# Grouping the distance-bias blocks of a two-layer hybrid block on TensorE: 12 groups instead of 32 single blocks, and 86 work tiles in SBUF

## Chip, cores and metric

The kernel runs on one core of one Trainium2 chip. The metric is the device time of one execution in microseconds, the median of three runs.

## What is computed

Two layers (`DEPTH = 2`) over one sequence of 512 tokens with model width 1024. Each layer makes a projection of the normed input, three branches (latent attention "mla", a chunked state-space branch "ssd", and a top-k attention "dsa"), gates and merges them, and adds a gated per-layer embedding. The change touches only the bias of the top-k attention, which depends on nothing but `positions` and the table `rel_bias`:

```python
def t5_bucket(rel):
    n = jnp.maximum(rel, 0)
    exact = REL_BUCKETS // 2
    log_ratio = jnp.log(jnp.maximum(n, exact).astype(jnp.float32) / exact) / math.log(REL_MAX_DIST / exact)
    large = jnp.minimum(exact + (log_ratio * (REL_BUCKETS - exact)).astype(jnp.int32), REL_BUCKETS - 1)
    return jnp.where(n < exact, n, large)

def dsa_branch(q_c, k_c, v_c, q_idx, k_idx, w_idx, positions, rel_bias):
    ...
    for blk in range(s // Q_BLOCK):                     # 4 query tiles of 128
        ...
        rel = jax.nn.relu(jnp.einsum('bqhd,bkd->bqhk', q_idx[:, qs:qe], k_idx))
        index_score = jnp.einsum('bqh,bqhk->bqk', w_idx[:, qs:qe], rel)
        index_score = jnp.where(key_ids <= q_ids, index_score, -jnp.inf)
        _, sel = lax.top_k(index_score, n_sel)          # n_sel = 128
        ...
        logits = jnp.einsum('bqhd,bqkd->bhqk', q_c[:, qs:qe], k_sel) * scale
        bucket = t5_bucket(positions[:, qs:qe, None] - pos_sel)
        logits = logits + jnp.moveaxis(rel_bias[bucket], -1, 1)
        probs = jax.nn.softmax(jnp.where(valid[:, None], logits, -jnp.inf), axis=-1)
        outs.append(jnp.einsum('bhqk,bqkd->bqhd', probs, v_sel))
```

The first query tile has only 128 keys before it, so it selects all of them; the other three need the top 128 of 256, 384 and 512.

## The kernel before

**Engines and order.** Everything is written as generators in `layer`. The order of TensorE is the order in which the code is run (a manual schedule); the other engines' instructions are put in order by the framework, which sets each as early as it thinks its inputs will be there, with a priority that follows the program's order (weight loads get a priority ahead, `AHEAD`). Once set, every engine works strictly in its order, and so do the DMA issues on SP (SyncE). Working tiles of 128x512 come from a ring of `NSLOT = 80` numbered slots; PSUM has eight banks under four tags, `BANKS = dict(mm=3, lg=2, tp=2, pv=1)`.

**Weights.** A matrix is brought by a DMA on SP (L225), split into a high part by ACT (L226, `wh`) and a low part by DVE (L227, `wl`); one tile of 128x512 outputs is then 24 matmuls of 128x512: `wh` and `wl` on the high input in turn (L237, L238), then `wh` on the low input (L245).

**The bias, layer 0 only.** `rel_bias` makes the bias of all 8 heads for the causal part of the 512x512 map in 32 blocks of 16 queries, from block 31 down to 0. A block has n = 512, 384, 256 or 128 key columns, eight blocks of each. For a block there are four masks of 128 x n (row = bucket and query, 1 where the distance reaches the bucket's limit): some on ACT by Sign (L379), the others on DVE by a comparison (L381); `SIGNS = (1, 2, 4)` says how many of the four ACT makes. Twelve bf16 matmuls follow (L393): three parts of the table's steps, times four masks, each to its own 32 of the 128 partitions of one PSUM bank. ACT takes the bank out (L397, the "eviction"), SP writes it to the DRAM tensor `bias_d` (L400). The masks of the next block are made while this one is multiplied.

**Where blocks are run.** `EARLY = (2, 0, 2, 2)` blocks stand between the steps of the layer's start. `REL = (1, 3, 4, 4)` stand in the four weaves of the mla attention, `LATE = 14` in the weave that holds the top-k selection (`TOP = (3, 22)`). A weave steps its main generator n times, and after each step runs a side track as long as that track's spent cost is under its share of its total:

```python
while t[2] and t[1] < t[0] * (i + 1) / n:
    t[1] += next(t[2][0])
```

What is left of a track after the n steps is run at the end, one after another. A block tells the cost 3n/512; the weave counts 2 for each block as the total.

**The top-k stage.** `topk` runs 16 rounds on DVE over the three later query tiles (L858 finds the eight largest, L861 strikes them out), then turns each score tile into an additive mask (L865, tiles `sel`). The side work of TensorE in this weave are 24-matmul tiles (`q_c`, `gate_c`, `merge`, `br_a`).

**Its attention, `dsa`.** For each head and query tile: SP reads the bias back from `bias_d` (L876), POOL adds the mask to it (L878: the causal mask `c` for the first query tile, `sel` for the others), TensorE makes the logits (L880, L881), `softmax` runs on DVE, ACT and DVE (L549 adds bias and logits, L550 exponential on ACT, L551, L552), TensorE transposes the probabilities (L560) and multiplies them with the values (L599). These reads run ahead of their use.

Of the kernel before, what the change touches and what calls it, by code (L numbers as in the profile page):

```python
# [27 lines left out]
BF = mybir.dt.bfloat16  # L28
I32 = mybir.dt.int32
AF = mybir.ActivationFunctionType  # L30
OP = mybir.AluOpType

L, D, T = 2, 1024, 512
# [125 lines left out]
class Build:  # L159
    def __init__(self, tc, I, out, ctx, dbg=None):  # L160
# [10 lines left out]
        self.dram = pool("dram", bufs=1, space=bass.MemoryType.DRAM)  # L171
        self.free_slots = deque(range(NSLOT))
        self.todo = deque()
# [8 lines left out]
    def slot(self, dt=F32, shape=(128, 512)):  # L182
        i = self.free_slots.popleft()
        self.peak = max(self.peak, NSLOT - len(self.free_slots))
        self.n += 1
# [180 lines left out]
    def rel_bias(self):  # L366


        nc = self.nc

        def masks(blk):
            n = 128 * (blk // 8 + 1)
            k = SIGNS[(blk < 32 - sum(EARLY)) + (blk < LATE)]
            tiles = [self.slot(BF, (128, 2, 512)) for _ in range(2)]
            for i in range(4):
                g = 4 * blk + i
                m = tiles[i // 2][:, i % 2, :n]
                if i >= 4 - k:
                    nc.scalar.activation(m, self.pk[:, :n], AF.Sign, scale=-1.0, bias=self.thr[:, 1, g:g + 1])  # L379
                else:  # L380
                    nc.vector.tensor_scalar(m, self.pk[:, :n], self.thr[:, 0, g:g + 1], None, op0=OP.is_le)  # L381
            return n, k, tiles
        nxt = masks(31)
        for blk in reversed(range(32)):
            n, k, tiles = nxt
            if blk:
                nxt = masks(blk - 1)
            else:
                self.rel(self.pk)
            ps = self.ps("mm" if blk >= 32 - sum(EARLY) else "tp")  # L390
            for s in range(3):
                for i in range(4):
                    nc.tensor.matmul(ps[32 * i:32 * i + 32, :n], self.steps[s][:, int(i >= 4 - k)],  # L393
                                     tiles[i // 2][:, i % 2, :n], start=s == 0, stop=s == 2)
            self.rel(*tiles)
            e = self.slot()
            nc.scalar.activation(e[:, :n], ps[:, :n], AF.Identity, scale=8.0, bias=self.half[:, k:k + 1])  # L397
            dst = bass.AP(tensor=self.bias_d.tensor, offset=self.bias_d.offset + blk * 16 * T,
                          ap=[[T, 16], [T * T, 8], [1, n]])
            nc.sync.dma_start(dst, e[:, :n])  # L400
            self.rel(e)
            yield 3 * n / 512


    def stat_add(self, s, x, first, t=slice(0, T)):
# [728 lines left out]
    def layer(self, l, xs, s):  # L1134
# [3 lines left out]
        for _ in range(PLE0):  # L1138
            next(p, None)
        blocks(EARLY[0])  # L1140
        self.now(p)
        blocks(EARLY[1])
        p = self.ple(l, 1)
# [4 lines left out]
        for _ in range(POST[l]):  # L1148
            next(p, None)
        blocks(EARLY[2])  # L1150
        R = self.stat_rows(y)
# [9 lines left out]
        self.now(p)  # L1161
        blocks(EARLY[3])
        self.ahead = AHEAD
# [7 lines left out]
        for j in range(4):  # L1171
# [6 lines left out]
                    [(ab, 33), merge(0, 6), merge(0, 7)]][j]  # L1178
            rel = [(self.rb_block(), 2) for _ in range(REL[j])] if l == 0 else []
            self.weave(att, 16, work, rel)  # L1180
# [16 lines left out]
        work += [merge(1, m) for m in range(2)]  # L1197
        self.weave(tk, TOP[1], work, [(self.rb_block(), 2) for _ in range(LATE * (l == 0))])
        att = self.dsa(l)
# [174 lines left out]


TOP = (3, 22)
REL = (1, 3, 4, 4)
WB = (3, 3, 2)
NSLOT = 80
LAST = 3  # L1380
CHUNK = 4
FIRST = (("c_kv", 0), ("c_kv", 1), "C")
# [4 lines left out]
POST = (4, 1)  # L1387
URGENT = 300
URGENT2 = 100
EARLY = (2, 0, 2, 2)  # L1390
SIGNS = (1, 2, 4)
LATE = 14
BANKS = dict(mm=3, lg=2, tp=2, pv=1)
AHEAD = 3000

# [24 lines left out]
```

## Time and profile before

| | us |
|---|---|
| median of three runs | 1435.06 (1434.89 to 1435.16) |
| the profiled execution's own time | 1434.97 |
| span of its trace | 1433.2 |
| PE busy | 1404.6 (98%) |
| DVE busy | 1085.9 (76%) |
| ACT busy | 724.3 (51%) |
| POOL busy | 155.4 (11%) |
| mean granted TensorE clock | 0.998 |

PE is the matmul side of TensorE, DVE is VectorE, ACT is ScalarE, POOL is GpSimd, and SP issues the DMAs. All times in the trace count from the start of the span. The timeline gives an instruction's start, its duration, engine and line, what it writes and reads, the number merged into the row, and in brackets the idle time before it with what ended it. Matmuls are pipelined: a duration of 0.39 us is a latency, and what a matmul costs is the distance to the next start, 0.227 to 0.23 us at 128x512.

### The profile page before, as it was taken

Reading aid. Unit: us, or ns where it says so; the run is one execution under the profiler, and the core shown is the slowest. Engines: PE = TensorE matmul, PEld = TensorE weight load, DVE = VectorE, ACT = ScalarE, POOL = GpSimd, SP = SyncE. Lnnn points to the kernel's source line nnn. Section 1 sums busy time; section 2 is a strip of 40 time slices with the busy share of each in tenths; the row PEclk is TensorE's granted clock in tenths of the full one; section 3 lists DMA queues with packets and bytes.
Section 4 is the critical chain, followed back from the end, with each engine's and each line's share of the span. In section 5 each row is a group of like instructions: output and inputs, shape, how many; then the busy total and the mean of one; then the engine's idle time right before and its main releaser. Section 6 shows DMA issues by size and latency. Waiting matters only on the chain.

```text
span 1433.2 us, 20180 instructions
## 1 busy us (share of the span) xinstructions
PE 1404.6 (98%) x7261; PEld 1151.6 (80%) x7262; DVE 1085.9 (76%) x2227; ACT 724.3 (51%) x1384; POOL 155.4 (11%) x142
## 2 busy tenths in 40 slices
PE   6999999999999999999999999999999999999997
PEld 4878777788888788888888788888888888788886
DVE  7668886996887997654565697779988799865444
ACT  7557678525655443433345575642366554443333
POOL 1000000003120231000001000000322114110000
PEclk9999999999999999999999999999999999999999
DMA  8442322343333332543454322233333343244331
GB/s 263 145 123 82 92 84 81 117 129 113 110 114 108 114 107 82 168 142 101 132 163 129 92 72 77 93 94 92 119 108 103 116 118 118 75 130 149 118 101 61
DMA packets 67609, 162.39 MB, mean 113 GB/s; under 512 B 9237, under 2 KB 21653, under 8 KB 67509
## 3 DMA queue, kind: packets, MB, share of 16 engines
q1 hardware_dynamic: 67509, 161.11, 36.1%
q8 instruction: 57, 0.93, 0.3%
q14 instruction: 43, 0.35, 0.1%
HBM read 142.27 MB, written 13.83 MB: 109 GB/s over the span
## 4 chain that ended last, share of the span: by engine, by line
PE 89%; DVE 6%; ACT 2%; issue 1%; SPq 0%; DMA 0%; POOL 0%; DVEq 0%; ACTq 0%
PE p L245 24%; PE p L237 24%; PE p L238 24%; PE p L599 3%; PE p L560 2%; DVE wl L227 1%; PE p L1070 1%; ACT wh L226 1%; PE p L1075 1%; DVE s L253 1%; PE p L680 1%; PE p L684 1%; PE p L681 1%; PE p L393 1%; PE p L1003 1%
## 5 line engine op out<-in xcount | busy, mean ns | idle before, releaser
L237 PE MATMUL p<-s,wh 128*128 128x512 f32 (+1 forms) x1644 | 648.8, 396 | 9.1 <-ACT wh L226 7.8
L238 PE MATMUL p<-s,wl 128*128 128x512 f32 (+1 forms) x1644 | 636.6, 388 | 1.2 <-DVE wl L227 1.2
L245 PE MATMUL p<-s,wh 128*128 128x512 f32 (+1 forms) x1644 | 424.4, 390 | 0.0
L226 ACT ACTIVATE wh<-wr 128x1024 fp32r<-128x1024 f32 (+2 forms) x214 | 223.5, 1044 | 326.0 <-PE p L245 212.3
L237 PEld LDWEIGHTS p<-s,wh 128*128 128x128 f32 x1644 | 309.7, 188 | 68.9 <-ACT wh L226 7.8
L238 PEld LDWEIGHTS p<-s,wl 128*128 128x128 f32 x1644 | 309.9, 189 | 60.5 <-DVE wl L227 2.6
L245 PEld LDWEIGHTS p<-s,wh 128*128 128x128 f32 x1644 | 300.6, 188 | 60.3 <-issue 2.8
L227 DVE TENSOR_TENSOR wl<-wr,wh 128x1024 fp32r<-128x1024 f32 (+2 forms) x214 | 266.7, 1246 | 101.7 <-ACT wh L226 100.2
L550 ACT ACTIVATE s<-s,m 128x128 f32<-128x128 f32 (+3 forms) x128 | 71.5, 559 | 66.1 <-DVE m L549 65.7
L569 ACT ACTIVATE s<-p 128x256 fp32r<-128x256 f32 (+1 forms) x192 | 66.0, 344 | 60.3 <-DVE s L570 31.1
L570 DVE TENSOR_TENSOR s<-p,s 128x256 fp32r<-128x256 f32 (+1 forms) x192 | 71.8, 374 | 16.2 <-ACT s L569 14.7
L878 POOL TENSOR_TENSOR s<-s,s 128x256 f32<-128x256 f32 (+2 forms) x48 | 58.9, 1244 | 204.8 <-ACT wh L226 60.2
L1129 DVE SCALAR_TENSOR_TENSOR s<-s,p 128x512 f32<-128x512 f32 x48 | 32.6, 678 | 35.9 <-PE p L245 35.9
L560 PE MATMUL p<-c,s 128*128 128x128 f32 x320 | 56.3, 274 | 2.2 <-DVE s L552 2.2
L410 ACT ACTIVATE s<-s 128x512 f32<-128x512 f32 (+1 forms) x42 | 25.3, 609 | 65.6 <-DVE s L1096 40.9
L560 PEld LDWEIGHTS p<-c,s 128*128 128x128 f32 x320 | 40.6, 140 | 18.5 <-issue 5.6
L552 DVE TENSOR_SCALAR s<-s,m 128x128 f32<-128x128 f32 (+3 forms) x128 | 53.5, 418 | 2.5
L963 DVE SCALAR_TENSOR_TENSOR s<-p,v,s 128x511 f32<-128x511 f32 (+2 forms) x72 | 53.3, 740 | 0.0
L861 DVE MATCH_REPLACE8 s<-m,s 128x256 f32<-128x256 f32 (+2 forms) x96 | 51.6, 542 | 0.0
L858 DVE MAX8 m<-s 128x8 f32<-128x256 f32 (+2 forms) x96 | 49.2, 547 | 0.0
L252 ACT ACTIVATE s<-s 128x512 fp32r<-128x512 f32 (+1 forms) x58 | 36.3, 626 | 25.5 <-DVE s L642 10.9
L253 DVE TENSOR_TENSOR s<-s,s 128x512 fp32r<-128x512 f32 (+1 forms) x58 | 43.2, 745 | 7.1 <-ACT s L252 6.7
(199 smaller groups left out, 1634.6 us busy)
## 6 DMA issues: line engine op xcount, KB each, us to landing
wr<-in_w_dram SPq DMA_DIRECT2D x204, 512.0 KB, 3.6
s<-cum_d SPq DMA_DIRECT2D x32, 256.0 KB, 3.8
s<-in_x_dram SPq DMA_DIRECT2D x16, 256.0 KB, 4.3
ple_d<-s SPq DMA_DIRECT2D x16, 256.0 KB, 4.1
s<-bias_d SPq DMA_DIRECT2D x16, 256.0 KB, 2.7
s<-ple_d SPq DMA_DIRECT2D x13, 256.0 KB, 2.7
s<-bias_d SPq DMA_DIRECT2D x16, 192.0 KB, 2.7
s<-s SPq DMA_DIRECT2D x44, 64.0 KB, 2.0
```

The source lines that it names most:

```text
L226: nc.scalar.activation(hi[:, :n], raw[:, :n], AF.Copy)
L227: nc.vector.tensor_sub(lo[:, :n], raw[:, :n], hi[:, :n].bitcast(F32))
L237: nc.tensor.matmul(ps[:, t], hi[:, c], ah[:, t], start=k == 0, stop=False)
L238: nc.tensor.matmul(ps[:, t], lo[:, c], ah[:, t], start=False, stop=False)
L245: nc.tensor.matmul(ps[:, t], hi[:, c], al[:, t], start=False, stop=k == n - 1)
L253: self.nc.vector.tensor_sub(lo, src, hi.bitcast(F32))
L550: nc.scalar.activation(u[:, :n], u[:, :n], AF.Exp, bias=mx, scale=-1.0, accum_out=sm)
L552: nc.vector.tensor_scalar(u[:, :n], u[:, :n], rs, None, op0=OP.mult)
L560: nc.tensor.transpose(tp[:, 128 * kb:128 * kb + 128], u[:, 128 * kb:128 * kb + 128], self.ident)
L569: nc.scalar.activation(h_, src, AF.Copy)
L570: nc.vector.tensor_sub(l_, src, h_.bitcast(F32))
L878: nc.gpsimd.tensor_tensor(b[:, :n], b[:, :n], mask, OP.add)
```

## The change

`masks` and the loop work on groups of neighbouring blocks of one width instead of single blocks. `GROUPS` has eight groups of two blocks (31 to 16) and four groups of four (15 to 12, 11 to 8, 7 to 4, 3 to 0). A group's matmuls run one block after another, with as many blocks side by side in a bank as fit in 512 columns; banks are taken in turn under the tags `tp` and `mm`. A bank is taken out by one eviction whatever is in it, and written by one DMA for each block. The number of matmuls (384), masks (128) and DMAs (32) stays; the evictions go from 32 to 22. `EARLY` is one group where it was two blocks, `REL` is (1, 1, 2, 2) groups, `LATE` is 3, `EDGES` sets the widths at which ACT takes over masks (blocks 13 and 12 have now two masks on ACT instead of four), and a group tells its cost as 3n times its blocks over 512, while the weave goes on counting 2 for each. `NSLOT` is 86.

```diff
--- before.py
+++ after.py
@@ -368,38 +368,47 @@
 
         nc = self.nc
 
-        def masks(blk):
-            n = 128 * (blk // 8 + 1)
-            k = SIGNS[(blk < 32 - sum(EARLY)) + (blk < LATE)]
-            tiles = [self.slot(BF, (128, 2, 512)) for _ in range(2)]
-            for i in range(4):
-                g = 4 * blk + i
-                m = tiles[i // 2][:, i % 2, :n]
-                if i >= 4 - k:
-                    nc.scalar.activation(m, self.pk[:, :n], AF.Sign, scale=-1.0, bias=self.thr[:, 1, g:g + 1])
+        def masks(group):
+            n, k = 128 * (group[0] // 8 + 1), SIGNS[(group[0] < EDGES[0]) + (group[0] < EDGES[1])]
+            per = 1024 // n
+            tiles = [self.slot(BF, (128, 1024)) for _ in range(-(-4 * len(group) // per))]
+            at = lambda m: tiles[m // per][:, n * (m % per):n * (m % per) + n]
+            for m in range(4 * len(group)):
+                g = 4 * group[m // 4] + m % 4
+                if m % 4 >= 4 - k:
+                    nc.scalar.activation(at(m), self.pk[:, :n], AF.Sign, scale=-1.0, bias=self.thr[:, 1, g:g + 1])
                 else:
-                    nc.vector.tensor_scalar(m, self.pk[:, :n], self.thr[:, 0, g:g + 1], None, op0=OP.is_le)
-            return n, k, tiles
-        nxt = masks(31)
-        for blk in reversed(range(32)):
-            n, k, tiles = nxt
-            if blk:
-                nxt = masks(blk - 1)
+                    nc.vector.tensor_scalar(at(m), self.pk[:, :n], self.thr[:, 0, g:g + 1], None, op0=OP.is_le)
+            return n, k, tiles, at
+        nxt = masks(GROUPS[0])
+        for j, group in enumerate(GROUPS):
+            n, k, tiles, at = nxt
+            if j + 1 < len(GROUPS):
+                nxt = masks(GROUPS[j + 1])
             else:
                 self.rel(self.pk)
-            ps = self.ps("mm" if blk >= 32 - sum(EARLY) else "tp")
-            for s in range(3):
-                for i in range(4):
-                    nc.tensor.matmul(ps[32 * i:32 * i + 32, :n], self.steps[s][:, int(i >= 4 - k)],
-                                     tiles[i // 2][:, i % 2, :n], start=s == 0, stop=s == 2)
+
+            banks, side = [], 512 // n
+            for b, blk in enumerate(group):
+                if b % side == 0:
+                    banks.append(self.ps(("tp", "mm")[len(banks) % 2]))
+                ps = banks[-1][:, n * (b % side):n * (b % side) + n]
+                for s in range(3):
+                    for i in range(4):
+                        nc.tensor.matmul(ps[32 * i:32 * i + 32], self.steps[s][:, int(i >= 4 - k)], at(4 * b + i),
+                                         start=s == 0, stop=s == 2)
             self.rel(*tiles)
-            e = self.slot()
-            nc.scalar.activation(e[:, :n], ps[:, :n], AF.Identity, scale=8.0, bias=self.half[:, k:k + 1])
-            dst = bass.AP(tensor=self.bias_d.tensor, offset=self.bias_d.offset + blk * 16 * T,
-                          ap=[[T, 16], [T * T, 8], [1, n]])
-            nc.sync.dma_start(dst, e[:, :n])
-            self.rel(e)
-            yield 3 * n / 512
+            for b0 in range(0, len(group), side):
+                blks = group[b0:b0 + side]
+                e, m = self.slot(), n * len(blks)
+                nc.scalar.activation(e[:, :m], banks[b0 // side][:, :m], AF.Identity, scale=8.0,
+                                     bias=self.half[:, k:k + 1])
+                for b, blk in enumerate(blks):
+                    dst = bass.AP(tensor=self.bias_d.tensor, offset=self.bias_d.offset + blk * 16 * T,
+                                  ap=[[T, 16], [T * T, 8], [1, n]])
+                    nc.sync.dma_start(dst, e[:, n * b:n * b + n])
+                self.rel(e)
+            yield 3 * n * len(group) / 512
 
 
     def stat_add(self, s, x, first, t=slice(0, T)):
@@ -1374,9 +1383,9 @@
 
 
 TOP = (3, 22)
-REL = (1, 3, 4, 4)
+REL = (1, 1, 2, 2)
 WB = (3, 3, 2)
-NSLOT = 80
+NSLOT = 86
 LAST = 3
 CHUNK = 4
 FIRST = (("c_kv", 0), ("c_kv", 1), "C")
@@ -1387,9 +1396,13 @@
 POST = (4, 1)
 URGENT = 300
 URGENT2 = 100
-EARLY = (2, 0, 2, 2)
+
+GROUPS = [list(range(a - 1, a - 1 - k, -1)) for a, k in
+          [(32 - 2 * i, 2) for i in range(8)] + [(16, 4), (12, 4), (8, 4), (4, 4)]]
+EARLY = (1, 0, 1, 1)
 SIGNS = (1, 2, 4)
-LATE = 14
+EDGES = (26, 12)
+LATE = 3
 BANKS = dict(mm=3, lg=2, tp=2, pv=1)
 AHEAD = 3000
 
```

Lines from L411 on move by 9, so what was L878 is now L887, L876 is L885, L865 is L874, L880 is L889; the matmuls L393 are L398, the evictions L397 are L404, the writes L400 are L409.

**TensorE at the first logits of `dsa`** (`p` is PSUM, `rbp` the table's steps, `wh` and `wl` a weight's parts, `s` slots). Before:

```order
L245 MATMUL p750_3760<-s82_413,wh748_3754 128x512
L245 MATMUL p750_3760<-s85_418,wh748_3754 128x512
L245 MATMUL p750_3760<-s88_423,wh748_3754 128x512
L245 MATMUL p750_3760<-s91_428,wh748_3754 128x512
L880 MATMUL p753_3793<-s152_806,s609_2898 128x256
L881 MATMUL p753_3793<-s153_807,s609_2898 128x256
L237 MATMUL p759_3810<-s69_392,wh757_3804 128x512
L238 MATMUL p759_3810<-s69_392,wl757_3805 128x512
```

After:

```order
L398 LDWEIGHTS rbp2_119
L398 MATMUL p710_3685<-s707_3613,rbp2_119 32x128
L398 LDWEIGHTS rbp2_119
L398 MATMUL p710_3685<-s707_3613,rbp2_119 32x128
L889 MATMUL p713_3743<-s154_812,s613_3000 128x256
L890 MATMUL p713_3743<-s155_813,s613_3000 128x256
L237 MATMUL p719_3760<-s71_398,wh717_3754 128x512
L238 MATMUL p719_3760<-s71_398,wl717_3755 128x512
```

The last two groups (96 matmuls, blocks 7 to 0) now stand directly ahead of the first logits; before, 152 rows lay between the last block and the logits.

**POOL at the adds of `dsa` in layer 0** (`c_77` is the causal mask of the first query tile; the other last operands are the three top-k masks). Before:

```order
L878 TENSOR_TENSOR s752_3790<-s752_3790,c_77 128x128
L878 TENSOR_TENSOR s786_3936<-s786_3936,c_77 128x128
L878 TENSOR_TENSOR s824_4108<-s824_4108,c_77 128x128
L878 TENSOR_TENSOR s760_3823<-s760_3823,s258_1280 128x256
L878 TENSOR_TENSOR s796_3980<-s796_3980,s258_1280 128x256
L878 TENSOR_TENSOR s767_3853<-s767_3853,s259_1281 128x384
L878 TENSOR_TENSOR s778_3897<-s778_3897,s260_1282 128x512
L878 TENSOR_TENSOR s804_4021<-s804_4021,s259_1281 128x384
```

After:

```order
L887 TENSOR_TENSOR s720_3773<-s720_3773,s264_1308 128x256
L887 TENSOR_TENSOR s756_3930<-s756_3930,s264_1308 128x256
L887 TENSOR_TENSOR s727_3803<-s727_3803,s265_1309 128x384
L887 TENSOR_TENSOR s738_3847<-s738_3847,s266_1310 128x512
L887 TENSOR_TENSOR s764_3971<-s764_3971,s265_1309 128x384
L887 TENSOR_TENSOR s774_4011<-s774_4011,s266_1310 128x512
L887 TENSOR_TENSOR s793_4100<-s793_4100,s264_1308 128x256
L887 TENSOR_TENSOR s802_4145<-s802_4145,s265_1309 128x384
L887 TENSOR_TENSOR s813_4189<-s813_4189,s266_1310 128x512
L887 TENSOR_TENSOR s712_3740<-s712_3740,c_77 128x128
L887 TENSOR_TENSOR s746_3886<-s746_3886,c_77 128x128
```

The adds of the first query tile stood ahead of nine adds that read the top-k masks; now they stand behind them.

**SP at the last writes to `bias_d` and the first reads of the first query tile** (`wr` are weights; `16x8x128` is a write of one narrow block). Before:

```order
L400 DMA bias_d_146<-s693_3419 16x8x128
L400 DMA bias_d_146<-s697_3441 16x8x128
L225 DMA wr733_3662<-in_w_dram 128x1024
L400 DMA bias_d_146<-s705_3491 16x8x128
L876 DMA s752_3790<-bias_d_146 128x128
L876 DMA s786_3936<-bias_d_146 128x128
L876 DMA s824_4108<-bias_d_146 128x128
L225 DMA wr739_3705<-in_w_dram 128x1024
```

After:

```order
L225 DMA wr752_3904<-in_w_dram 128x1024
L225 DMA wr770_3989<-in_w_dram 128x1024
L885 DMA s813_4189<-bias_d_146 128x512
L225 DMA wr789_4074<-in_w_dram 128x1024
L409 DMA bias_d_146<-s709_3679 16x8x128 x4
L409 DMA bias_d_146<-s711_3734 16x8x128 x4
L885 DMA s712_3740<-bias_d_146 128x128
L885 DMA s746_3886<-bias_d_146 128x128
```

The eight narrow writes now stand together, behind weight loads that stood behind them before; the 128x128 reads stand behind all eight.

## Rows read from the trace of the kernel before

**Rows 1.** The page, busy time of each engine: us (share of the span) xinstructions.

```profile
PE 1404.6 (98%) x7261; PEld 1151.6 (80%) x7262; DVE 1085.9 (76%) x2227; ACT 724.3 (51%) x1384; POOL 155.4 (11%) x142
```

**Rows 2.** Windows: busy us of each engine, granted clock, DMA share, GB/s.

```profile
312.00:322.00 10.00, 10.00 (x46) 8.26 (x44) 10.00 (x24) 1.44 (x2) 0.34 (x1) 1.00 0.38 135
```

**Rows 3.** Timeline of PE, bias runs: the first in a weave, and the last.

```profile
106.06 0.83 PE L393 MATMUL p<-s,rbp 128*32 128x512 bf16 x12
...
292.53 0.35 PE L393 MATMUL p<-s,rbp 128*32 128x128 bf16 x12
```

**Rows 4.** Timeline of PE, a run of two narrow blocks and one of one.

```profile
276.05 0.39 PE L238 MATMUL p<-s,wl 128*128 128x512 f32 x1
276.36 0.52 PE L393 MATMUL p<-s,rbp 128*32 128x128 bf16 x24
...
277.15 0.39 PE L238 MATMUL p<-s,wl 128*128 128x512 f32 x1
...
284.65 0.39 PE L238 MATMUL p<-s,wl 128*128 128x512 f32 x1
284.96 0.35 PE L393 MATMUL p<-s,rbp 128*32 128x128 bf16 x12
...
285.59 0.40 PE L238 MATMUL p<-s,wl 128*128 128x512 f32 x1
```

**Rows 5.** Timeline of PE near the start: a wait for an eviction.

```profile
20.55 0.50 PE L237 MATMUL p<-s,wh 128*128 128x512 f32 x1 [1.08 <-ACT s L397]
```

**Rows 6.** Line L397, the evictions: count, ns min/median/max, first and last start.

```profile
L397 ACT ACTIVATE s<-p,rbh x32: 352/524/696, 17.1 to 292.9; 128x512 f32<-128x512 f32 x8, 128x384 f32<-128x384 f32 x8, 128x256 f32<-128x256 f32 x8, 128x128 f32<-128x128 f32 x8
```

**Rows 7.** Timeline of DVE: top-k's first and last instructions, then the first softmax.

```profile
252.75 0.43 DVE L858 MAX8 m<-s 128x8 f32<-128x256 f32 x1
...
321.24 0.90 DVE L865 TENSOR_SCALAR s<-s 128x256 f32<-128x256 f32 x3
...
327.98 0.29 DVE L549 CUSTOM_DVE_ANT_0 s<-p,s 128x128 f32<-128x128 f32 x1 [3.46 <-PE p L881]
...
328.73 1.23 DVE L227 TENSOR_TENSOR wl<-wr,wh 128x1024 fp32r<-128x1024 f32 x1 [0.45 <-ACT wh L226]
...
330.07 0.57 DVE L552 TENSOR_SCALAR s<-s,m 128x128 f32<-128x128 f32 x1
```

**Rows 8.** Timeline of POOL, 296 to 334 us: its bias adds.

```profile
297.95 2.28 POOL L878 TENSOR_TENSOR s<-s,c 128x128 f32<-128x128 f32 x3 [162.80 <-DMA s<-bias_d]
321.66 11.12 POOL L878 TENSOR_TENSOR s<-s,s 128x256 f32<-128x256 f32 x9 [21.43 <-issue]
```

**Rows 9.** Line L878: its first-query-tile adds, ns min/median/max.

```profile
L878 POOL TENSOR_TENSOR s<-s,c x16: 460/466/1322, 297.9 to 1101.8; 128x128 f32<-128x128 f32 x16
```

**Rows 10.** Timeline of PE: the first logits, and the first transpose of probabilities.

```profile
327.44 0.28 PE L880 MATMUL p<-s,s 128*128 128x256 f32 x1
...
332.50 0.27 PE L560 MATMUL p<-c,s 128*128 128x128 f32 x1
```

**Rows 11.** Line L400, the bias writes: ns of an issue; us from issue to landing.

```profile
L400 SPq DMA_DIRECT2D bias_d<-s x32: 517/528/790, 18.0 to 293.3; - x32
...
DMA to landing us min/median/max: 2.2/3.1/5.2
```

**Rows 12.** Line L876, the bias reads: us from issue to landing.

```profile
DMA to landing us min/median/max: 1.7/2.7/4.8
```

**Rows 13.** Timeline of PE at the start, after 7.84 us without work.

```profile
7.84 0.79 PE L237 MATMUL p<-s,wh 128*128 128x512 f32 x1 [7.84 <-ACT wh L226]
...
9.69 0.63 PE L237 MATMUL p<-s,wh 128*128 128x512 f32 x1
...
13.11 0.93 PE L245 MATMUL p<-s,wh 128*128 128x512 f32 x2
```

**Rows 14.** Timeline of PE, its last instruction.

```profile
1425.10 0.43 PE L435 MATMUL p<-c,m 128*128 128x128 f32 x2
```

**Rows 15.** Windows behind it: the column after the five engines is the granted clock.

```profile
1427.00:1427.50 0.50, 0.00 (x0) 0.00 (x0) 0.50 (x2) 0.00 (x0) 0.36 (x1) 0.50 0.00 0
```

## What the change was expected to do

> **What bounds the kernel now.** I read the page first: PE is busy for 98% of the span, DVE 76%, ACT 51%, POOL 11% [rows 1]. So a microsecond taken from TensorE's stream is worth a microsecond, unless the stream then has to wait. I then read the windows, to see whether another engine is full anywhere. In the stretch of the top-k selection DVE is busy 10.00 of 10 us [rows 2], from the first MAX8 at 252.75 to the last mask at 321.24 + 0.90 = 322.14 [rows 7], while PE is full too. That is a second chain as long as PE's: the masks come when DVE is through, however fast PE is. Last I read the timeline from the end of top-k to the first attention of `dsa`. There PE makes the first logits at 327.44 and transposes the first probabilities at 332.50 [rows 10] without idle time before it. The bias adds of the first query tile were done on POOL long before, from 297.95; the nine adds that need the masks ran from 321.66 for 11.12 us [rows 8]. So before the change the first probabilities hung on nothing late.
>
> **What is removed from PE.** In the weaves there are 23 runs of bias matmuls, the first at 106.06 and the last at 292.53 [rows 3]. The change leaves 8 there, so 15 fewer. What a run costs I read where a run of two narrow blocks and a run of one stand near each other. From the weight matmul ahead of the run to the second one behind it, two blocks take 277.15 - 276.05 = 1.10 us, one takes 285.59 - 284.65 = 0.94 [rows 4]. Without a run these two steps are 0.46, so a run of two costs 0.64, of one 0.48: each narrow block 0.16, and 0.32 for going in and out. The blocks' own time stays; 15 x 0.32 = 4.8. Runs that end at a 128-column transpose, not at a weight matmul, pay a little less on leaving, so I take 4.6, with 3.9 and 5.0 as ends. **The ten evictions less** I price at nothing: ACT is at 51% [rows 1] and its evictions run beside TensorE's weight matmuls; without that cover they would be worth 10 x 0.52 = 5.2 at the median [rows 6].
>
> **What is added: two evictions to wait for.** A group of two wide blocks fills two banks, and the next user of the second bank waits for one eviction more. Near the start PE already waits 1.08 us for an eviction [rows 5], and a 512-wide one lasts 0.67 to 0.70, the median one 0.52 [rows 6]. For the three early groups I take 0.8 together (0 to 1.4: none, or two more evictions in full). Two later groups of 384-wide blocks are followed, four transposes on, by a matmul that takes the bank: two evictions are 1.05, the transposes cover about 0.55, so 0.5 each at most; I take 0.4 each, ends 0 and 0.5. Together 1.6, ends 0 and 2.4. The `q_c` tiles ahead of top-k move with PE, so top-k starts 1.6 us later. The masks that move from ACT to DVE are four of 256 columns, made before top-k; at the 0.43 of a DVE instruction of that width [rows 7] they are 1.7 us of an engine that is at 76%, and I price them at nothing, since TensorE's work ahead of their group covers them.
>
> **What is moved.** Three orders change together, and the rest of the forecast hangs on them.
>
> First, DVE. Between top-k's first instruction and its last stands one weight split more than before, 1.23 us by the one at 328.73 [rows 7]. So the first of the nine adds, at 321.66 before, starts at 321.66 + 1.6 + 1.2 = 324.5.
>
> Second, POOL. The nine adds with masks now stand ahead of the first query tile's. In the timeline they took 11.12 us [rows 8]. While they ran, DVE ran two weight splits with two inputs from SBUF, one of them the 1.23 at 328.73 [rows 7]; after the change one stands there. If each split held POOL up in full, the adds alone are 8.7 us and with one split 9.9; if none did, 11.1. I take 9.9. Then the first tile's add, 0.47 [rows 9]: 324.5 + 9.9 + 0.5 = 334.9. From the start of the softmax on DVE to its last multiply the timeline has 327.98 to 330.64, of which one split is 1.23 [rows 7]; that split is not between them any more, but the exponential on ACT still is, so between 1.4 and 2.7; I take 1.9. First transpose at 336.8, against 332.50: 4.3 us later.
>
> The Trainium skill ("SBUF — State Buffer", section "SBUF: two separate sides") says that GpSimd and a VectorE instruction with two SBUF inputs exclude each other for a whole instruction. By that rule the adds take 9.9 and the time is the forecast below; without it they take 11.1, and the time is 1.2 longer. The merged row of nine adds neither shows nor denies it.
>
> Third, SP and PE. Blocks 7 to 0 now end right ahead of the first logits. A group of cost 6 uses up the whole track's share in the top-k weave (3 x 2), so the last two groups are left for the weave's end. PE gets there at 327.44 - 4.6 + 1.6 = 324.4. The last eviction ends about 0.8 later; eight writes at 0.52 an issue [rows 11], four of which can start behind the first of the two groups, put the last issue at about 328.2; 3.1 us to landing [rows 11], 2.7 for the read [rows 12], and add and softmax as above: 334.0 + 0.5 + 1.9 = 336.4. Before, these writes were over by 293 us and cost nothing. So two roads, one over POOL and one over DRAM, lead to the same late time. Undoing one of them alone would gain little.
>
> PE comes to the first transpose at 332.50 - 4.6 + 1.6 = 329.5 and waits there some 7.3 us. Nothing on PE can pass it. Weights are not late behind it: two splits stand ahead of the softmax on DVE, which is enough for 11 us of matmuls.
>
> **The clock.** PE's last matmuls start at 1425.10 [rows 14], and two microseconds later the granted clock is at 0.50, the lower of the two levels [rows 15]. So a wait of 7 us should end at 1.2 GHz. At the kernel's start, after 7.84 us without work, eight matmuls from 9.69 to 13.11 take 0.43 each [rows 13] where they take 0.23 later. So coming back costs 8 x 0.20 = 1.6 at least, and (13.11 - 7.84)/2 = 2.6 if every microsecond since the first matmul counts as half lost; I take 2.0.
>
> The Trainium skill's page "TensorE: Matmul & The Clock Gate" ("Why this matters for your kernels") asks for no idle gaps between bursts of matmuls, since they bring the lower clock back. It speaks against this change, and the trace agrees where it can be seen, 0.50 behind PE's last work.
>
> **Sum.** Up to the transpose 4.3 later (the 4.6 saved is used up in the wait), plus 2.0 for the clock: 6.3 on the profiled execution's 1434.97, which lies at the median of the three runs (1435.06). Forecast 1441.3. Its ends: with no early loss, adds of 8.7 and a softmax of 1.4 the transpose is at 321.7 + 1.2 + 8.7 + 0.5 + 1.4 = 333.5, plus 1.0; with 1.6 for the clock 1437.6. With 2.4 early, adds of 11.1, an add of 0.8 and 2.7: 339.9, plus 7.4; with 2.6 for the clock 1445.0.
>
> **The rivals.**
>
> *The clock holds through the wait.* For it: no wait of that length lies in the middle of this trace. Against it: the lower clock two microseconds after PE's last work [rows 14, 15]. Time 1434.97 + 4.3 = 1439.3.
>
> *The transfers set the end.* If the last write takes its longest landing, 5.2, and the read 4.8, both seen, the transpose comes at 336.4 + 2.1 + 2.1 = 340.6, 8.1 late; with the clock 1445.1. For it: eight writes come in one burst beside weight loads. Against it: medians are 3.1 and 2.7.
>
> *The wait is short.* If top-k starts no later than before and the adds are quick, and the clock stays, only the 1.0 of the low end is left: about 1436.0, no change that can be told.
>
> *The saving stays (not slower).* If the first query tile's bias is there when PE comes, the change gives 1434.97 - 4.6 + 1.6 = 1432.0. It decides by one point: that bias must be ready 2.4 us ahead of 329.5, at 327.1. For it: everything PE saves is real and no other wait is new. Against it: POOL's order, in which nine adds that cannot begin before 321.7 stand ahead.
>
> **How the numbers follow.** Forecast 0.52, clock holds 0.17, transfers 0.08, short wait 0.14, saving stays 0.09. About 0.2% (2.9 us) is what a measurement of this kernel can tell from no change: faster is below 1432.2, slower above 1437.9. The saving-stays case is faster (0.08, a little of it on the line); the short wait and some of the edges of the others are the same (0.17); the rest is slower (0.75). The range leaves out the saving-stays case and the far ends: 1435 to 1446.
>
> **What would show it.** In the trace after: a PE wait of 5 to 10 us ahead of the first L569, put down to DVE's L561; POOL's first 128x128 add behind nine others, at about 334; the last of the L409 writes landing past 330; matmul steps of 0.43 for a few microseconds behind the wait; layer 1 unchanged. PE should reach the first logits some 3 us earlier than 327.44. I am wrong if the first query tile's add runs before the masks, if the wait is under 3 us, or if PE makes up the time later in layer 0.

## The result, and the profile after

The changed kernel took 1452.61 us (median of five runs, 1448.72 to 1454.02) against 1435.09 before (1434.89 to 1435.20): a ratio of 1.0119, 95% interval 1.0106 to 1.0132. It is slower, as forecast, but by 17.5 us and not by 6.3; the time lies outside the range. The profiled execution took 1454.01 with a span of 1452.2, so its trace has to account for 19.0 us over the 1434.97 before.

The page, busy time of each engine, answers [rows 1]:

```profile
PE 1408.8 (97%) x7262; PEld 1159.6 (80%) x7262; DVE 1085.3 (75%) x2231; ACT 720.8 (50%) x1370; POOL 152.4 (10%) x142
```

No engine has more work. TensorE, with 4.4 us less to do in the bias runs of the weaves, is busy for 4.2 us longer, for the most part because some of its work ran at the lower clock (below), and the rest of the 19 us is idle time. The waits of PE over the whole span (line that waited, what for: total us, times, longest):

```profile
PE p L569 <- DVE m L560: 7.7, 1, 7.7
PE p L444 <- POOL m L437: 4.0, 2, 3.7
PE p L569 <- DVE s L561: 3.3, 4, 1.3
PE p L608 <- DVE s L579: 3.2, 4, 1.1
...
PE p L237 <- ACT s L404: 1.8, 1, 1.8
...
PE p L398 <- ACT s L404: 0.8, 1, 0.8
```

The first is the one the prediction spoke of. The second, at L444, it did not know, and the third and fourth have grown by 1.1 and 2.1 us.

To see where the time went I took the start of the same matmul in both traces (the order of everything but the bias blocks is the same on PE) and read how far the new kernel is behind:

| stretch of the trace before | forecast | measured | of it lower clock |
|---|---|---|---|
| to 36 us: waits for second evictions | +0.8 | +2.3 | 1.6 |
| 61 to 74 us: L444 | 0 | +5.6 | 1.6 |
| 74 us to the first logits: fewer runs, later waits | -3.8 | -3.7 | |
| first transpose of probabilities: the wait | +7.3 | +7.9 | |
| behind it | +2.0 | +2.1 | 2.1 |
| rest of layer 0 | 0 | +3.3 | 1.5 |
| layer 1 | 0 | +1.8 | |
| sum | +6.3 | +19.3 | |

(The traces begin at slightly different points, hence 19.3 and not 19.0.) Three lines are right to within a microsecond, four are not.

**The late probabilities.** POOL, SP and PE at the first attention of `dsa`, answering [rows 8], [rows 11] and [rows 10]. POOL's timeline:

```profile
331.15 10.15 POOL L887 TENSOR_TENSOR s<-s,s 128x256 f32<-128x256 f32 x9 [187.47 <-DVE s L874]
342.33 1.37 POOL L887 TENSOR_TENSOR s<-s,c 128x128 f32<-128x128 f32 x3 [1.03 <-DMA s<-bias_d]
```

SP's timeline, the eight narrow writes and the reads behind them:

```profile
333.15 5.57 SPq L409 DMA_DIRECT2D bias_d<-s  x8
340.46 7.85 SPq L885 DMA_DIRECT2D s<-bias_d  x6
```

PE's timeline:

```profile
330.06 1.52 PE L398 MATMUL p<-s,rbp 128*32 128x128 bf16 x96
331.51 0.38 PE L889 MATMUL p<-s,s 128*128 128x256 f32 x1
...
344.57 0.44 PE L569 MATMUL p<-c,s 128*128 128x128 f32 x1 [7.73 <-DVE m L560]
...
347.16 0.63 PE L237 MATMUL p<-s,wh 128*128 128x512 f32 x1
347.59 0.63 PE L238 MATMUL p<-s,wl 128*128 128x512 f32 x1
```

The nine adds come first and end at 341.30; then the first query tile's add still waits 1.03 us for the read that follows the eight writes. Both roads of the prediction are there, a microsecond apart. PE stands for 7.73 us, and the steps behind it are 347.59 - 347.16 = 0.43 us, half speed. All of this is what was forecast; only it happens 8 us later than forecast.

**The early wait.** DVE's timeline before, at the second norm (it takes the statistic of `c_kv`, 128x4, at L427; L641 is the product with `sin` for the rotary part of the keys):

```profile
57.48 0.15 DVE L427 TENSOR_SCALAR m<-p 128x4 f32<-128x4 f32 x1
62.13 0.81 DVE L641 TENSOR_TENSOR s<-s,sin 32x512 f32<-32x512 f32 x1 [4.49 <-DMA sin<-rope_d]
```

And after (L427 is L436, L641 is L650):

```profile
63.64 0.68 DVE L650 TENSOR_TENSOR s<-s,sin 32x512 f32<-32x512 f32 x1 [5.71 <-DMA sin<-rope_d]
...
66.27 0.15 DVE L436 TENSOR_SCALAR m<-p 128x4 f32<-128x4 f32 x1
```

The framework has put the two the other way round. The statistic could be taken at about 59.7, when TensorE's sums were there, but DVE stood at the product, which waits for a DMA until 63.64. Nothing of this is in the changed code: the early blocks only come in other places of the program, and the list of DVE's instructions was dealt out anew. POOL's power and TensorE's transposes L444 (L435 before) follow from the statistic; PE did not wait for them before and waits 3.73 us after:

```profile
61.87 0.60 PE L435 MATMUL p<-c,m 128*128 128x128 f32 x4
```

```profile
68.07 0.65 PE L444 MATMUL p<-c,m 128*128 128x128 f32 x4 [3.73 <-POOL m L437]
```

Windows of the changed kernel (granted clock behind the five engines, 1.00 is 2.4 GHz, 0.50 is 1.2), of that stretch, of the one behind the wait at the probabilities and of one at 416 us:

```profile
68.00:73.00 5.00, 4.93 (x17) 4.02 (x18) 4.24 (x6) 2.09 (x4) 0.87 (x4) 0.66 0.70 207
73.00:80.00 7.00, 7.00 (x33) 5.77 (x32) 2.37 (x4) 2.18 (x3) 0.26 (x1) 1.00 0.20 74
344.00:349.00 5.00, 4.42 (x12) 3.68 (x13) 2.74 (x7) 2.58 (x8) 1.08 (x2) 0.50 0.08 27
416.00:419.00 3.00, 2.31 (x10) 1.96 (x11) 2.39 (x8) 1.36 (x4) 0.46 (x1) 0.75 0.14 48
```

The clock fell behind this wait, behind the wait at 344, and again at 416 behind two waits of 1.20 and 0.45 us. By the comparison of starts a fall cost 1.5 to 2.1 us each time. It had also fallen behind the 1.81 us wait at 21 us.

### The profile page after: what moved, and what is told of

It reads as the page before. It is cut to its first block, busy times and chain, and to the rows that moved or that the text cites. A ratio compares the mean times of both kernels' runs of the same rounds, so it can differ in the third digit from the quotient of the medians.

```text
span 1452.2 us, 20165 instructions
## 1 busy us (share of the span) xinstructions
PE 1408.8 (97%) x7262; PEld 1159.6 (80%) x7262; DVE 1085.3 (75%) x2231; ACT 720.8 (50%) x1370; POOL 152.4 (10%) x142
## 4 chain that ended last, share of the span: by engine, by line
PE 82%; DVE 11%; ACT 3%; issue 2%; DMA 1%; SPq 0%; POOL 0%; DVEq 0%; ACTq 0%; POOLq 0%
PE p L237 22%; PE p L245 22%; PE p L238 22%; PE p L608 3%; DVE wl L227 2%; PE p L569 2%; DVE s L870 2%; DVE m L867 2%; PE p L1079 1%; PE p L1084 1%; ACT wh L226 1%; PE p L689 1%; PE p L690 1%; PE p L1012 1%; DVE s L253 1%
## 5 line engine op out<-in xcount | busy, mean ns | idle before, releaser
L237 PEld LDWEIGHTS p<-s,wh 128*128 128x128 f32 x1644 | 311.3, 189 | 69.4 <-ACT wh L226 7.8
L887 POOL TENSOR_TENSOR s<-s,s 128x256 f32<-128x256 f32 (+2 forms) x48 | 55.1, 1166 | 312.1 <-DVE s L874 194.5
L455 DVE SCALAR_TENSOR_TENSOR s<-s,v,p 128x512 f32<-128x512 f32 x42 | 29.0, 743 | 23.8 <-PE p L444 23.8
```

What stands on the lines that cost most here:

```text
L237: nc.tensor.matmul(ps[:, t], hi[:, c], ah[:, t], start=k == 0, stop=False)
L887: nc.gpsimd.tensor_tensor(b[:, :n], b[:, :n], mask, OP.add)
```

## The experiments

The theory from the trace: the time is lost in two places that add up, the first 74 us and the first attention of `dsa`, and something small besides, in the second halves of the two `dsa` stages. Since the early loss delays the tiles from which top-k starts, and DVE is full through top-k, it is not absorbed by the wait at the probabilities. The rivals are named with each run. Each run was timed beside the kernel before, which took 1435.57 us with runs 1, 2, 3 and 5, 1435.32 with 4, 6, 7 and 8 and 1435.10 with 9 and 10. The changed kernel's own five runs lie 5.3 us apart, so a difference to it is good to a microsecond or two and no better.

**1. The last groups earlier.** One number in the weave:

```diff
-        self.weave(tk, TOP[1], work, [(self.rb_block(), 2) for _ in range(LATE * (l == 0))])
+        self.weave(tk, TOP[1], work, [(self.rb_block(), 28 / 3) for _ in range(LATE * (l == 0))])
```

> The changed kernel, with one number altered: in the top-k weave each of the three late groups counts 28/3 instead of 2, so that the last two groups run in the first half of the weave, as the last blocks did before, and not at its end. Theory: the changed kernel lost its time in two places that add up, about 7.8 us in the first 73 us (an order on DVE and waits for evictions, with the clock lowered behind them), which also starts top-k late, and 8.0 us of waiting plus 2.2 for the clock at the first probabilities of dsa, because the last groups end late. This kernel should lose the second: no wait over 1 us ahead of the first L569, POOL's first-query-tile adds ahead of the nine, TensorE at that transpose some 3 us later than before, and 1438 to 1442 us in all. Rival: the late end of top-k (331 us against 322) alone holds the first probabilities back through the nine adds; then the wait stays at 5 us or more and the time is above 1445.

1442.56 us (1440.56 to 1442.87), ratio to before 1.0044 (1.0027 to 1.0060): 10.0 less than the changed kernel, and 0.6 above what was expected (1438 to 1442). POOL's first adds, and PE's first transpose, which has no idle time ahead of it any more:

```profile
292.43 1.70 POOL L887 TENSOR_TENSOR s<-s,c 128x128 f32<-128x128 f32 x3 [149.60 <-DMA s<-bias_d]
```

```profile
336.25 0.27 PE L569 MATMUL p<-c,s 128*128 128x128 f32 x1
```

It is 3.75 us later than [rows 10]. So the late end of top-k does not by itself hold the first probabilities: the rival falls. The second loss is the place of the last two groups.

**2. The first six blocks single.** Sizes and tags alone (the sizes are shown; the six banks come under the tag `mm`):

```diff
-          [(32 - 2 * i, 2) for i in range(8)] + [(16, 4), (12, 4), (8, 4), (4, 4)]]
-EARLY = (1, 0, 1, 1)
+          [(32 - i, 1) for i in range(6)] + [(26 - 2 * i, 2) for i in range(5)] + [(16, 4), (12, 4), (8, 4), (4, 4)]]
+EARLY = (2, 0, 2, 2)
```

> The changed kernel, with the first six blocks single again (12 groups become 17: six of one, five of two, three of four; EARLY 2, 0, 2, 2, and the six banks under the tag mm). The last groups still end at the end of the top-k weave. Theory: the early loss of 7.8 us goes (on DVE the second norm's statistic stands ahead of the product with sin again), top-k starts about as before, and what is left is what the prediction priced: a wait of 6 to 8 us ahead of the first L569, 2 us of half speed behind it, 1439 to 1445 us. Rival: the early part does not matter, since TensorE waits for the probabilities anyway and the time lost early is taken out of that wait; then 1449 or more, as the changed kernel.

1445.60 us (1444.60 to 1446.30), ratio 1.0063 (1.0048 to 1.0078): 7.0 less than the changed kernel, and 0.6 above what was expected (1439 to 1445). DVE's timeline in the early part, then PE's at the probabilities:

```profile
57.52 0.16 DVE L436 TENSOR_SCALAR m<-p 128x4 f32<-128x4 f32 x1
62.57 0.68 DVE L650 TENSOR_TENSOR s<-s,sin 32x512 f32<-32x512 f32 x1 [4.89 <-DMA sin<-rope_d]
```

```profile
336.47 0.44 PE L569 MATMUL p<-c,s 128*128 128x128 f32 x1 [7.43 <-DVE s L561]
```

The statistic stands ahead of the product again, although the slots are still 86, so it was the early groups that turned the two round. The early loss is gone, and the transpose starts at 336.47 after a wait of 7.43, where the prediction had 336.8 and 7.3. The wait did not grow when the early delay was taken out, which the rival asked for. This kernel is what the prediction priced, but for the last rows of the table, some 4 us.

**3. Both edits.**

> Both edits at once: the first six blocks single, and the late groups in the first half of the top-k weave. Groups of two and four stay for blocks 25 to 0. Theory: both losses go and the shorter time of the bias runs stays: 4.4 us less in the weaves by the trace, against 1 us or so of waits for second evictions: 1431 to 1434 us, faster than before. Rival: the saving is eaten elsewhere (the later waits of layer 0 and layer 1, together some 5 us in the changed kernel, come from the groups or the slots and not from the two places): 1435 to 1440.

1436.04 us (1434.69 to 1439.28), ratio 1.0005 (0.9995 to 1.0014). Both losses go, 16.6 of the 17.5 us, and add up as the theory has it (10.0 + 7.0). But the saving does not show: the expected 1431 to 1434 was missed and the rival was right, about 4 us are lost elsewhere. By the comparison of starts this kernel is 2.4 us ahead of before at 293 us and 1.1 behind at the end, with the losses at the transposes and products around 369, 1061 and 1091 us.

**4. The statistic of the second norm on ACT**, all else as changed:

```diff
-            nc.vector.tensor_scalar(v, ps[:, a:b], 1.0 / dim, EPS, op0=OP.mult, op1=OP.add)
+            if dim == 256:
+                nc.scalar.activation(v, ps[:, a:b], AF.Copy, scale=1.0 / dim, bias=EPS)
+            else:
+                nc.vector.tensor_scalar(v, ps[:, a:b], 1.0 / dim, EPS, op0=OP.mult, op1=OP.add)
```

> The changed kernel, with the second norm's statistic (scale and epsilon, 128x4) taken by ACT and not by DVE; all else as changed. Theory: of the early loss 5.5 us come from one place on DVE, where that statistic stands behind the product with sin, which waits for a DMA until 63.6 us; on ACT it waits for nothing there. So the wait of 3.7 us ahead of the transposes L444 falls below 1.5, the clock does not fall behind it, top-k starts 4 to 5 us earlier, and the time is 1446 to 1449.5. Rival: TensorE needs the weight split behind the same wait on DVE, so it stops there instead; 1451 or more.

1445.18 us (1443.59 to 1446.05), ratio 1.0067 (1.0053 to 1.0081): 7.4 less than the changed kernel, and 0.8 below what was expected (1446 to 1449.5). PE's transposes (here L447) have no idle time ahead of them:

```profile
62.33 0.60 PE L447 MATMUL p<-c,m 128*128 128x128 f32 x4
```

So one instruction of 128x4 behind one wait cost the early 5.6 us, the 1.6 of the clock behind that wait included. The profiled executions differ by 8.7 (1454.01 and 1445.34), and the other 3.1 are two falls of the clock: it did not fall at 21 us in this execution (below), nor at the place that was 416 us, where it is 1.00 behind waits of 1.2 and 0.5 us. The wait at the probabilities is 7.6 us, as in the changed kernel, which again shows that the early delay and that wait add.

**5. Only the slots.** The kernel before with 86:

```diff
-NSLOT = 80
+NSLOT = 86
```

> The kernel before with 86 slots instead of 80, and nothing else. Theory: the slots alone move some bias reads and adds but nothing on the path: 1434 to 1436 us. Rival: the slots set the orders that cost 3.3 us behind the first probabilities and 1.7 us in layer 1 of the changed kernel: 1437 to 1440.

1439.24 us (1436.86 to 1443.60), ratio 1.0024 (1.0015 to 1.0034). Nothing but the length of the ring has changed, and it costs 3.7 us; the rival was right. DVE, POOL and PE at 366 us:

```profile
365.91 2.32 DVE L227 TENSOR_TENSOR wl<-wr,wh 128x1024 fp32r<-128x1024 f32 x1
...
368.22 1.43 DVE L253 TENSOR_TENSOR s<-s,s 128x512 fp32r<-128x512 f32 x1
```

```profile
365.55 3.56 POOL L878 TENSOR_TENSOR s<-s,s 128x512 f32<-128x512 f32 x2 [8.68 <-DMA s<-bias_d]
```

```profile
372.11 0.63 PE L599 MATMUL p<-s,vc 128*128 128x256 f32 x3 [1.15 <-DVE s L570]
```

Another ring gives other reads and another order of the adds. Two adds of 512 columns now run beside a weight split and a split of activations on DVE. The weight split takes 2.32 us where [rows 7] has 1.23, the adds 3.56 for two where a single one takes 1.29 (at 356.11 us of the trace before), and the probabilities of that tile reach PE 1.15 us late. The same picture, with the same 2.32, stands in layer 1 at 1059 us. By the comparison of starts the two `dsa` stages lose 1.6 and 1.9 us. The profiled execution is 4.5 us behind; its other 0.9 lies at 62 us, where POOL's product with `cos` waited for its DMA until 60.27 us instead of 58.30, and this is not there in run 10, which has 86 slots too.

**6. POOL's road cut.** In the changed kernel the first query tile's adds of layer 0 go to DVE:

```diff
-            nc.gpsimd.tensor_tensor(b[:, :n], b[:, :n], mask, OP.add)
+            (nc.vector if qt == 0 and l == 0 else nc.gpsimd).tensor_tensor(b[:, :n], b[:, :n], mask, OP.add)
```

> The changed kernel, with the bias adds of the first query tile in layer 0 on DVE and not on POOL, so that they do not stand behind the nine adds with masks. Theory: two roads lead to the late probabilities, and in the changed kernel the one over DRAM is the later by 1.0 us (POOL was free at 341.3 and its first-tile add waited for the read until 342.3). So the wait ahead of the first L569 stays at 6 to 8 us, and the time is within 2 us of the changed kernel's 1452.6. Rival: POOL's order holds the probabilities back; the wait falls under 2 us and the time under 1446.

1451.33 us (1450.10 to 1453.16), ratio 1.0112 (1.0099 to 1.0126). DVE's add, and PE's wait:

```profile
340.05 0.29 DVE L887 TENSOR_TENSOR s<-s,c 128x128 f32<-128x128 f32 x1 [9.22 <-DMA s<-bias_d]
```

```profile
342.07 0.45 PE L569 MATMUL p<-c,s 128*128 128x128 f32 x1 [7.18 <-DVE m L560]
```

The add is free of the nine and waits for the read from DRAM instead; PE waits 7.18 us instead of 7.73. So undoing POOL's order alone gains nothing, as the prediction said of the two roads. The other road alone was not cut; by the rows of the changed kernel POOL was free at 341.30 and began at 342.33, so cutting it alone would have gained about 1.0 us, an estimate.

**7. A version from the parts that pay.** 80 slots, single wide blocks in their old places, groups of four for the narrow blocks only:

```diff
-REL = (1, 1, 2, 2)
+REL = (1, 3, 4, 3)
-NSLOT = 86
+NSLOT = 80
-          [(32 - 2 * i, 2) for i in range(8)] + [(16, 4), (12, 4), (8, 4), (4, 4)]]
-EARLY = (1, 0, 1, 1)
+          [(32 - i, 1) for i in range(16)] + [(16, 4), (12, 4), (8, 4), (4, 4)]]
+EARLY = (2, 0, 2, 2)
```

with 28/3 in the weave as in 1 and the tag `mm` for the six early banks.

> A version that keeps what the runs showed to pay: the kernel before's places, 80 slots and single blocks for the wide blocks 31 to 16, groups of four for the narrow ones (15 to 0), and the late groups in the first half of the top-k weave (EARLY 2, 0, 2, 2; REL 1, 3, 4, 3; 28/3 for each of three late groups). 14 runs in the weaves instead of 23. Theory: each run less is 0.3 us, nothing else moves, POOL's order is that of before: 2.9 us less than before, 1431.5 to 1433. Rival: top-k on DVE is as long as before, and what TensorE saves is waited out behind it: 1434.5 to 1436.

1432.71 us (1431.27 to 1434.28), ratio 0.9982 (0.9973 to 0.9991): the only version here that does all the work and is faster than the kernel before, by some 2.6 us. The 9 runs less in the weaves, at 0.3 each, come out whole, and the ten evictions less, which this version has too, add nothing, as the prediction had it. PE at the first transpose, against 332.50 in [rows 10]:

```profile
329.62 0.27 PE L569 MATMUL p<-c,s 128*128 128x128 f32 x1
```

It is 2.9 us earlier and nothing is waited out behind it, although top-k on DVE ends no earlier than in [rows 7]:

```profile
322.19 0.89 DVE L874 TENSOR_SCALAR s<-s 128x256 f32<-128x256 f32 x3
```

**8. 83 slots, with both edits of 3.**

> As the kernel with both edits (first six blocks single, late groups early), with 83 slots instead of 86. Theory: the slots decide when bias reads and POOL's adds run, and where an add meets two-input work on DVE both get slower (a split took 2.32 us beside an add of 512 columns, 1.21 without); with 86 slots this costs some 3.5 us in the second halves of the two dsa stages. With 83 it comes out otherwise: 1432 to 1434.5 if the adds fall beside it. Rival: the number of slots above 80 does not matter, only that the ring is longer: the same 1436 as with 86.

1434.45 us (1433.93 to 1435.37), ratio 0.9995 (0.9985 to 1.0004): 1.6 less than with 86 and still no gain on before. It lies at the upper edge of what was expected (1432 to 1434.5), and the intervals of the two ratios overlap, so the 1.6 is not sure. With 83 the losses at 369 and 1061 us stay (1.4 and 1.6 by the comparison of starts), the one at 1091 goes. Neither rival nor theory is settled by it; what the traces show is that each number of slots deals another order.

**9 and 10. The adds taken away.** The kernel before, with 80 and with 86 slots, without the mask adds of six heads:

```diff
-            nc.gpsimd.tensor_tensor(b[:, :n], b[:, :n], mask, OP.add)
+            if h < 2:
+                nc.gpsimd.tensor_tensor(b[:, :n], b[:, :n], mask, OP.add)
```

> The kernel before, without POOL's mask add for six of the eight heads (heads 2 to 7, both layers): the bias goes into the softmax as it is read, so masked keys are not masked there. It is the base for the next run. Theory: POOL's adds share something with DVE's two-input work, so without most of them DVE is a little quicker in dsa: 1432 to 1435. Rival: the adds touch nothing on the path: 1435, as before.

> The kernel before with 86 slots, without the same mask adds of heads 2 to 7. 86 slots alone cost 3.7 us with the adds. Theory: the loss comes from POOL adds that fall beside DVE's splits; without the adds 86 slots cost nothing: within 1 us of the run with 80 slots and no adds. Rival: the slots cost by the reads or by other orders on DVE, and the 3 us stay.

1430.08 us (1429.57 to 1430.91) with 80 slots and 1430.02 (1429.78 to 1430.29) with 86, ratios to before 0.9967 (0.9954 to 0.9979) and 0.9965 (0.9952 to 0.9978). With the adds, 86 slots cost 3.7 us; without, nothing. So it is the adds of POOL through which the slots cost, and even in the kernel before, taking three quarters of them away gains 5 us, more than was expected. By the comparison of starts the gain lies in the two `dsa` stages, 2.1 to 2.2 us in each. The page of the run with 80 slots shows where it comes from:

```profile
PE 1404.3 (98%) x7262; PEld 1152.2 (81%) x7262; DVE 1075.5 (75%) x2227; ACT 725.0 (51%) x1384; POOL 104.8 (7%) x94
```

DVE runs the same 2227 instructions as in [rows 1] and is busy for 10.4 us less: weight splits, splits of activations and the last multiply of the softmax are shorter by 3.4 to 3.6 us each in sum. With the adds and 86 slots it is busy for 1083.8 us, no more than with 80. So the slots do not lengthen DVE's work in sum; they move where it is held up. In the six heads the softmax waits neither for an add nor for the top-k mask any more, and how much of the 5 us that gives, no run shows.

The Trainium skill ("SBUF — State Buffer", section "SBUF: two separate sides") says that GpSimd and a VectorE instruction with two inputs in SBUF hold a shared pair of ports in turn, each for its whole instruction. The rows agree: the split took 2.32 instead of 1.23, 1.1 us more, within the time of one 512-wide add. Taken in turn from 365.55, an add of 1.29, the split of 1.23 and an add of 1.29 would end at 366.84, 368.07 and 369.36, an estimate; the split ended at 365.91 + 2.32 = 368.23 and the second add at 365.55 + 3.56 = 369.11.

## Why the prediction was wrong, step by step

- **Fewer runs, 4.6 us (3.9 to 5.0).** Right. The eight runs of the weaves cost 11.5 us where the 23 cost 15.9, by the steps around them: 4.4. The 96 matmuls of the last run begin at 330.06 and the logits behind them at 331.51, the narrow blocks' own time and 0.3.
- **Two evictions to wait for, 1.6 us (0 to 2.4).** Half right, half luck. The three early groups cost 0.7 (2.3 at 36 us less the clock's 1.6), where 0.8 was taken. What was missed is that the wait at 21 us brought the clock down, for another 1.6 in this execution. The 0.8 for the two later groups came out in size alone: after 36 us PE waits for no eviction L404, and the 0.7 by which -3.7 falls short of the 4.4 shows mostly at products L608, which now wait for DVE. The eight at 158 us before (L599) and after:

```profile
157.67 1.20 PE L599 MATMUL p<-s,s 128*128 128x256 f32 x8
```

```profile
165.98 1.94 PE L608 MATMUL p<-s,s 128*128 128x256 f32 x8
```

- **The early part as a whole.** This is the step that failed. The prediction showed the order of three engines at the end of top-k and priced the start from the evictions alone. It did not look at DVE's order between 36 and 74 us, where no line of the change stands, and where it had moved; 5.6 us were lost there, against a forecast of nothing, and top-k moved with them. The start of top-k was forecast 1.6 us late; it was 261.33 against 252.75 in [rows 7], 8.6 late:

```profile
261.33 0.43 DVE L867 MAX8 m<-s 128x8 f32<-128x256 f32 x1
...
330.73 0.89 DVE L874 TENSOR_SCALAR s<-s 128x256 f32<-128x256 f32 x3
```

- **One split more in top-k, 1.2 us.** From the first MAX8 to the first mask 330.73 - 261.33 = 69.4 us, against 321.24 - 252.75 = 68.5 in [rows 7]: 0.9.
- **The nine adds, 9.9 us.** 10.15, right, and nearer to the 9.9 of one split that holds POOL up than to the 11.1 of none. **The road over DRAM.** From the end of the last run to the transpose 12.0 forecast, 13.1 measured; the eight writes took 5.57 us to issue instead of 4.2.
- **The wait, 7.3 us, and the clock, 2.0.** 7.73 and 2.1. With the early part put right (run 2) PE comes to the first logits at 323.70, forecast 324.4, and the transpose starts at 336.47, forecast 336.8.
- **Nothing behind it.** Wrong: 86 slots were not priced at all. They alone cost 3.7 us (run 5), spread over both layers, through POOL's adds (runs 9 and 10); the fall of the clock at 416 us added 1.5 in the profiled execution. "Layer 1 unchanged" was wrong for that reason.

The terms left out, 7.1 at the start (7.9 less the 0.8 forecast) and 5.1 behind, are 12.2 of the 13.0 us by which the trace is behind the forecast (19.3 less 6.3). The mechanism that was forecast was there, with its size, and by run 1 it was the largest single loss, 10.0 us; it was not the only one.

What stays open: single runs of the changed kernel lie up to 5 us apart, those of before on the same chip 0.3. The clock fell four times in the profiled execution, and in that of run 4 it held at two of these places; each fall is 1.5 to 2.1 us. The mean granted clock of the single runs goes with their times: 0.992 in the three slowest (1452.61 to 1454.02), 0.994 in the other two (1448.72 and 1451.11). By these rounded shares the difference of 0.002 is some 3 of the 5 us, an estimate. What makes the clock fall in one run and hold in the next stays open.

## What to carry to other kernels

Where a scheduler orders the engines, a change in one place can deal out the others' orders anew: compare the order of every engine over the whole program, above all for short instructions that now stand behind a wait for a DMA, and not only where the changed lines are. Take a change apart before judging it: here 12 groups, their places and 6 more slots came as one edit, and the part that pays (narrow blocks side by side in the old places, 2.6 us) was hidden under three that cost 10, 7 and 4. A delay ahead of a stage in which another engine is full is not absorbed by a wait behind that stage, since the stage moves as a whole.

## What the runs showed of the hardware that was not expected

Short waits of TensorE can lower its clock, and need not. Near 21 us PE waited 1.81 us in the changed kernel and 1.95 in that of run 4, each behind a wait of 1.4 to 1.8 us some four microseconds earlier, and what came after differed. The windows of the changed kernel and of run 4:

```profile
20.00:25.00 5.00, 3.94 (x10) 3.11 (x11) 4.34 (x10) 3.93 (x7) 0.00 (x0) 0.66 0.86 308
```

```profile
20.00:25.00 5.00, 4.16 (x20) 3.54 (x21) 4.88 (x11) 4.83 (x9) 0.00 (x0) 1.00 0.84 308
```

Half of the matmuls stand in the first (10 against 20), at a mean granted clock of 0.66; in the second it held at 1.00. The fall cost about as much as the wait itself, 1.6 us. In runs 1 and 6, whose code there is the changed kernel's own, it held as well; run 6, behind waits of 1.76 and 1.80 us:

```profile
20.00:25.00 5.00, 3.77 (x19) 3.19 (x20) 5.00 (x11) 4.83 (x10) 0.00 (x0) 1.00 0.88 315
```

At 416 us waits of 1.20 and 0.45 us stand in the changed kernel and, at 414, in run 6, where the clock fell (0.75 in both), and waits as long in run 4, where it held.

A POOL add of 512 columns and a weight split on DVE that meet cost each other about a microsecond (2.32 against 1.23, 3.56 for two adds), and taking away three quarters of the adds made the kernel before 5 us faster, though POOL is busy for only 11% of the span. It is not only DVE's work with two tiles as inputs that is held up: the multiply L552, of one tile and a factor for each row, took 1.42 us at 371.29 beside an add that began at 371.12 in the trace before, and 0.48 at 373.92 in run 5, where no add ran beside it.
